# Scan of a chunked delta rule: float16 splits of state, values and updates made in halves of two heads

## The chip, the cores and the metric

The kernel runs on one core of a Trainium2 chip. The metric is the device time of one execution in microseconds (us), the median of several runs. The engines are called PE (TensorE matmul), PEld (TensorE weight load), DVE (VectorE), ACT (ScalarE), POOL (GpSimd) and SP (SyncE, here the queue that issues most transfers).

## The reference

One inference layer over 128 context tokens and 2048 latent tokens, model width 1024. Each token is normalised, modulated and projected; three branches of width 512 mix the tokens, are gated, projected and merged. The change is in branch A, a bidirectional gated delta rule with 4 heads of 128 x 128 state:

```python
def step(s, inp):
    u0_, w_, qk_, qg_, kd_, gl_ = inp
    u = u0_ - jnp.einsum('bhck,bhkv->bhcv', w_, s)
    o = jnp.einsum('bhck,bhkv->bhcv', qg_, s) + jnp.einsum('bhij,bhjv->bhiv', qk_, u)
    s = gl_[..., None, None] * s + jnp.einsum('bhck,bhcv->bhkv', kd_, u)
    return s, o
...
o_f, s_f = gated_delta_chunked(q, k, v, g[:, :, 0], beta[:, :, 0], s0_f)
o_b, s_b = gated_delta_chunked(rev(q), rev(k), rev(v), rev(g[:, :, 1]), rev(beta[:, :, 1]), s0_b)
```

`u0_` and `w_` come from a triangular solve within a chunk.

## The kernel before, in words

Every product is made in float16 pairs: an operand is written as a high part (`hi`, its cast) and a low part (`lo`, the remainder), and `mm3` (through `mm`, line 161, the line of nearly all TensorE rows) adds hi x hi, hi x lo and lo x hi. `split` (lines 900 to 902) makes such a pair from a float32 tile of 128 x 512, which holds four heads of 128 columns: ScalarE casts all of it (line 901), then VectorE makes the remainder of all of it (line 902).

`scan` runs 34 steps: 17 chunks of 128 tokens forward (`d` = 0), then 17 backward (`d` = 1), the context's chunk first in each. A step is a chain through four engines:

- `kT_` (tile `sk`) times the state pair `S16` goes to a PSUM bank; VectorE subtracts it from the values `v_` (tile `sv`), one head at a time (line 973); `split` gives `v16`.
- `v16` times `R`, the chunk's inverse, goes to a bank; VectorE multiplies by beta (line 995); `split` gives `u`.
- `kn16` times `u` goes to a bank; VectorE adds it to the decayed state `S`, one head at a time (line 1012); `split` gives the next `S16`.

In the profile the tiles carry names without digits: `v`, `u`, `S`, `kn` and `sk`. Beside the chain, `level` makes `R` for later chunks, `attend` the outputs `o`, and `finish` normalises them. In the first direction no split of S follows the last chunk; in all there are 34 splits of v, 34 of u and 32 of S.

The scan is a generator. `Pace` (lines 306 to 335) advances it while the weight products of the other branches and of the merge are written out, so that those cover the chain. The order in the program is then changed once more: the kernel is built under a scheduler that works out by its own timing which instruction each engine takes next (`schedule_with_timeline_sim=True`). On the chip each engine runs its list in that order and waits at its head.

Two other users of ScalarE's queue matter. `converting` loads a weight block (tile `wst`) and squares it (line 209) for its scale, then casts it (line 218, `whi` or `bhi`); VectorE makes the remainder (line 219). `branch_block` casts another branch's rows (line 1334, tile `big`), which arrive by transfer too.

Of the kernel before, what the change touches and what calls it, by code (L numbers as in the profile page):

```python
# [11 lines left out]
F16 = mybir.dt.float16  # L12
I32 = mybir.dt.int32
BF16 = mybir.dt.bfloat16
AF = mybir.ActivationFunctionType
ALU = mybir.AluOpType
# [4 lines left out]
P = 128  # L21
# [6 lines left out]
H = 4  # L28
WB = 512
# [8 lines left out]
FS = 4096.0  # L38
# [73 lines left out]
def hybrid_flow_kernel(ctx: ExitStack, tc: tile.TileContext, x_prompt, x_sample, state_delta, c, c_ctx, ln_g, w_ada,  # L112
# [3 lines left out]
    V, A, G, PE, SY = nc.vector, nc.scalar, nc.gpsimd, nc.tensor, nc.sync  # L116
    uid, rot = [0], [0]

    def nm(s):
        uid[0] += 1  # L120
        return f"{s}_{uid[0]}"

    def pool(stack, name, bufs, **kw):
        return stack.enter_context(tc.tile_pool(name=name, bufs=bufs, **kw))

    def sb(pl, shape, tag, dt=F32, bufs=None):
        kw = {} if bufs is None else {"bufs": bufs}
        return pl.tile(list(shape), dt, tag=tag, name=nm(tag), **kw)
# [11 lines left out]
    def bank(pl, shape, tag="b"):  # L140
        if pl is ps_d:
            rot[0] += 1
            pl = ps_d[rot[0] % 3]
        return pl.tile(list(shape), F32, tag=tag, name=nm(tag))
# [18 lines left out]
    def mm3(out, l, r):  # L163

        mm(out, l[0], r[0], True, False)
        mm(out, l[0], r[1], False, False)
        mm(out, l[1], r[0], False, True)
# [224 lines left out]
    for blk in range(8):  # L392
# [3 lines left out]
        ps = bank(ps_d, [2, 256])  # L396
# [41 lines left out]
    for ti, (t0, tn) in enumerate(TBS):  # L438
# [13 lines left out]
        for k in range(KT):  # L452
            ps = bank(ps_d, [P, tn])
            for j in range(nt):
                PE.transpose(ps[:, j * P:(j + 1) * P], xt[:, j, k * P:(k + 1) * P], ident)
            t = sb(p0p, [P, tn], "xm", bufs=3)
# [3 lines left out]
        for g in range(4):  # L460
            ps = bank(ps_d if tn == P and g % 2 else ps_mm, [P, tn])
# [12 lines left out]
    def h3(ap):  # L474
        return ap.rearrange("p (h x) -> p h x", h=H)
# [5 lines left out]
    beta, eg, egl, ed, neg = [sb(dp, dsh, n_) for n_ in ("beta", "eg", "egl", "ed", "neg")]  # L481
# [5 lines left out]
    dq = pool(dl, "dqa", 1, side="right")  # L487
# [118 lines left out]
    for ct in range(12):  # L606
        w = getw(1, 2 if ct < 6 else min(4, 15 - ct))
        for half in range(1):
# [4 lines left out]
            for t0, tn in TBS:  # L613
                flip[0] ^= 1
                ps = bank(ps_d if flip[0] else ps_mm, [P, tn])
                gemm_T(ps, w, 0, xh[:, :, t0:t0 + tn], xl[:, :, t0:t0 + tn])
                o = t0 + 1 if t0 < NS else t0 + 3
# [31 lines left out]
    hs = lambda h: slice(h * P, (h + 1) * P)  # L649
# [4 lines left out]
    def bc(col, n):  # L654
        return col.rearrange("p (h o) -> p h o", o=1).to_broadcast([P, H, n])
# [241 lines left out]

    pair = lambda t_, h: (t_[:, 0, hs(h)], t_[:, 1, hs(h)])

    def split(t_, src, scale=1.0):  # L900
        A.activation(t_[:, 0, :], src, AF.Copy, scale=scale)
        V.scalar_tensor_tensor(t_[:, 1, :], src, scale, t_[:, 0, :], ALU.mult, ALU.subtract)

    def attend(d, t, S, u, qk_, qT_):
        o = sb(dq, [P, WB], "o")
        if S is not None:
            ps = bank(ps_out, [P, WB])
            for h in range(H):
                mm3(ps[:, hs(h)], pair(qT_, h), pair(S, h))
            for h in range(H):  # L910
                A.activation(o[:, hs(h)], ps[:, hs(h)], AF.Copy, scale=eg[:, d, t, h:h + 1])
        yield 1
        ps = bank(ps_out, [P, WB])
        for h in range(H):
            mm3(ps[:, hs(h)], pair(qk_, h), pair(u, h))
        if S is not None:
            for h in range(H):
                V.scalar_tensor_tensor(o[:, hs(h)], ps[:, hs(h)], rq[:, t, h:h + 1], o[:, hs(h)], ALU.mult, ALU.add)
        else:
            V.tensor_tensor(h3(o), h3(ps), bc(rq[:, t, :], P), ALU.mult)  # L920
        yield 1
        if d == 0:
            SY.dma_start(ofD[t], o)
        else:
            yield from finish(t, o)

    def scan():
        order = [(d, s_, t) for d in range(2) for s_, t in enumerate([16] + (list(range(16)) if d == 0 else list(range(15, -1, -1))))]

        def step_loads(i):  # L930

            if i == len(order):
                return None
            d, s_, t = order[i]
            kT_ = None
            if s_:
                kT_ = sb(dq, [P, 2, WB], "sk", F16)
                SY.dma_start(kT_, kTD[t])
            kn_ = sb(dq, [P, WB], "skn")
            SY.dma_start(kn_, kvD[t][:, 0, :])  # L940
            v_ = sb(dq, [P, WB], "sv")
            SY.dma_start(v_, kvD[t][:, 1, :])
            return kT_, kn_, v_

        loaded = step_loads(0)
        lev = level(0, 16)
        R = next(lev)
        for _ in range(14):
            yield 1
        for i in range(3):  # L950
            next(lev)
            if i == 1:
                nlev = level(*order[1][::2])
                R2 = next(nlev)
            for _ in range(3):
                yield 1
        att = iter(())
        for i_, (d, s_, t) in enumerate(order):
            if s_ == 0:
                S = S16 = None  # L960
                S0 = sb(dq, [P, WB], "S")
                SY.dma_start(h3(S0), state_delta[0, 0, d].rearrange("h k v -> k h v"))
            kT_, kn_, v_ = loaded
            G.tensor_tensor(h3(kn_), h3(kn_), bc(ed[:, d, t, :], P), ALU.mult)
            kn16 = sb(dq, [P, 2, WB], "kn16", F16)
            A.copy(kn16[:, 0, :], kn_)
            G.tensor_tensor(kn16[:, 1, :], kn_, kn16[:, 0, :], ALU.subtract)
            if S is not None:
                ps = bank(ps_chain, [P, WB])
                for h in range(H):  # L970
                    mm3(ps[:, hs(h)], pair(kT_, h), pair(S16, h))
                for h in range(H):
                    V.scalar_tensor_tensor(v_[:, hs(h)], ps[:, hs(h)], neg[:, d, t, h:h + 1], v_[:, hs(h)], ALU.mult, ALU.add)  # L973
            v16 = sb(dq, [P, 2, WB], "v16", F16)
            split(v16, v_)
            next(lev, None)
            yield 1
            next(att, None)
            yield 1
            next(nlev, None)  # L980
            yield 1
            next(lev, None)
            yield 1
            next(att, None)
            yield 1
            qk_ = sb(dq, [P, 2, WB], "sqk", F16)
            qT_ = None
            if S is not None:
                qT_ = sb(dq, [P, 2, WB], "sq_", F16)
                SY.dma_start(qT_, qTD[t])  # L990
            SY.dma_start(qk_, qkD[d][t])
            ps = bank(ps_chain, [P, WB])
            for h in range(H):
                mm3(ps[:, hs(h)], [R[:, h, l].rearrange("p b c -> p (b c)") for l in range(2)], pair(v16, h))
            V.tensor_tensor(h3(v_), h3(ps), bc(beta[:, d, t, :], P), ALU.mult)
            u = sb(dq, [P, 2, WB], "u", F16)
            split(u, v_)
            yield 1
            next(nlev, None)
            yield 1  # L1000
            next(att, None)
            yield 1
            last = s_ == 16
            S2 = S216 = None
            if not last:
                ps = bank(ps_chain, [P, WB])
                for h in range(H):
                    mm3(ps[:, hs(h)], pair(kn16, h), pair(u, h))
                if S is not None:
                    S2 = S  # L1010
                    for h in range(H):
                        V.scalar_tensor_tensor(S2[:, hs(h)], S[:, hs(h)], egl[:, d, t, h:h + 1], ps[:, hs(h)], ALU.mult, ALU.add)
                else:
                    st = sb(dq, [P, WB], "of")
                    A.activation(st, ps, AF.Copy, scale=bnds[:, 3:4])
                    SY.dma_start(new_state[0, 0, d].rearrange("h k v -> k h v"), h3(st))
                    S2 = S0
                    V.tensor_scalar(S2, S2, us, FS, ALU.mult, ALU.mult)
                S216 = sb(dq, [P, 2, WB], "S16", F16, bufs=2)
                split(S216, S2, 1.0 / FS)  # L1020
            yield 1
            next(nlev, None)
            lev, nlev = nlev, level(*order[i_ + 2][::2]) if i_ < 32 else iter(())
            loaded = step_loads(i_ + 1)
            R3 = next(nlev, None)
            yield 1
            yield 1
            for _ in att:
                pass
            yield 1  # L1030
            att = attend(d, t, S16, u, qk_, qT_)
            S, S16, R, R2 = S2, S216, R2, R3
        for _ in att:
            yield 1
# [111 lines left out]
    ps = bank(ps_x, [P, 4, P])  # L1146
# [21 lines left out]
    for t in range(NCH):  # L1168
        ps = bank(ps_mm, [P, 4, P])
# [30 lines left out]
    for g in range(4):  # L1200
# [5 lines left out]
        for ti, (t0, tn) in enumerate(TBS):  # L1206
            st = vrow[:, t0:t0 + tn]
            ps = bank(ps_mm, [P, tn])
# [17 lines left out]
    for g in range(4):  # L1226
        xw, zw = getw(2, 2)
        for gh in range(1):
# [18 lines left out]
            for q in range(0, NCH, 4):  # L1247
                qn = min(4, NCH - q)
                ps = bank(ps_mm, [P, qn, P])
                for i in range(qn):  # L1250
                    t = q + i
# [42 lines left out]
            for q4 in range(5):  # L1294
# [8 lines left out]
                if q4 == 2:  # L1303
                    ps = bank(ps_x, [P, P])
# [180 lines left out]
    for i_, t in enumerate(order):  # L1485
# [11 lines left out]
        for i, (c0, c1) in enumerate([(0, 512), (512, 896), (896, D)] if end else [(0, 512), (512, D)]):  # L1497
            cs = slice(c0, c1)
            ps = bank(ps_mm, [P, c1 - c0])
# [53 lines left out]
```

## Time and profile before

| | |
|---|---|
| median of 3 runs | 2205.27 us (2204.06 to 2205.95) |
| profiled execution | 2200.86 us, span 2199.1 us |
| mean granted TensorE clock | 0.994 |
| PE busy | 2135.7 us, 97% |
| DVE, ACT, POOL busy | 59%, 46%, 32% |
| the scan | about 900 to 1720 us |

A row of a group gives line, engine, operation, tiles out<-in, shapes and count, then busy time, mean ns of one, and the idle time of the engine just before with what ended it. A row of a timeline gives the start in us, the duration in us, engine, line, operation, tiles, shapes and count, and in brackets the idle time before it. Matmuls overlap, so the distance between starts, not the duration, is what one costs.

### The profile page before, as it was taken

How to read it: one execution, taken by the hardware profiler on the slowest of the kernel's cores; microseconds unless marked ns; L12 is line 12 of the kernel's file. 1: busy time of each engine (PE TensorE's matmuls, PEld its weight loads, DVE VectorE, ACT ScalarE, POOL GpSimd, SP SyncE). 2: the span in 40 equal slices, each digit the busy share in tenths (PEclk: the TensorE clock that was granted, in tenths of full speed). 3: DMA queues.
4: the chain of work that ended last, by engine and by line, in shares of the span. 5: the costliest groups of instructions: out<-in, count | busy, mean ns of one | idle time of the engine just before them, and what ended most of it. 6: DMA issues, size and time to landing. Idle time of an engine off the chain costs nothing.

```text
span 2199.1 us, 41985 instructions
## 1 busy us (share of the span) xinstructions
PE 2135.7 (97%) x15990; PEld 1232.4 (56%) x15990; DVE 1299.4 (59%) x3085; ACT 1006.6 (46%) x2325; POOL 713.9 (32%) x861
## 2 busy tenths in 40 slices
PE   7999999999899999999899999999999999999998
PEld 3564444455455588878555556555655444444444
DVE  5736755479879696455665555756574544233454
ACT  3545644455555563344644445655653422222332
POOL 1421433223334322432321223355443222122553
PEclk8999999999999999999999999999999999999999
DMA  8434733176777754433755556756664544333542
GB/s 281 145 94 162 253 111 110 60 214 212 243 224 233 209 161 115 118 122 115 220 175 164 163 160 189 240 183 209 213 203 147 172 125 128 119 101 118 174 151 105
DMA packets 304275, 365.04 MB, mean 166 GB/s; under 512 B 39393, under 2 KB 215754, under 8 KB 302026
## 3 DMA queue, kind: packets, MB, share of 16 engines
q1 hardware_dynamic: 251690, 267.38, 39.8%
q0 software_dynamic: 12688, 51.27, 6.5%
q10 hardware_dynamic: 39696, 43.72, 6.0%
q8 instruction: 125, 2.05, 0.4%
q14 instruction: 76, 0.62, 0.1%
HBM read 234.67 MB, written 127.62 MB: 165 GB/s over the span
## 4 chain that ended last, share of the span: by engine, by line
PE 48%; DMA 7%; DVE 4%; ACT 4%; issue 2%; POOL 1%; ACTq 1%; SPq 0%; POOLq 0%; DVEq 0%
PE b L161 47%; DMA wst<-in_w_branch_dram 1%; DMA st<-br 1%; DMA wst<-in_w_in_dram 1%; ACTq L672 1%; POOL st L1133 1%; DMA br<-o 1%; DMA skn<-kv 0%; DMA ei<-XB 0%; DVE sv L973 0%; DVE wlo L219 0%; ACT big L1334 0%; DMA mrow<-mrg 0%; ACT nd L739 0%; DMA XB<-nd 0%
## 5 line engine op out<-in xcount | busy, mean ns | idle before, releaser
L161 PE MATMUL b<-xh,whi 128*128 128x512 f16 (+1 forms) x1920 | 649.5, 347 | 4.7 <-DVE sg L1123 3.0
L161 PE MATMUL b<-xl,whi 128*128 128x512 f16 (+1 forms) x1920 | 650.0, 347 | 0.0
L161 PE MATMUL b<-xh,wlo 128*128 128x512 f16 (+1 forms) x1920 | 649.2, 347 | 0.2 <-DVE wlo L219 0.2
L161 PEld LDWEIGHTS <-whi 128*128 128x128 f16 x3904 | 355.9, 98 | 330.3 <-issue 8.7
L161 PEld LDWEIGHTS <-wlo 128*128 128x128 f16 x1952 | 190.8, 98 | 178.6 <-issue 0.7
L161 PE MATMUL b<-big,bhi 128*128 128x512 f16 (+1 forms) x960 | 250.8, 348 | 1.0 <-DVE big L1335 1.0
L1374 POOL TENSOR_TENSOR mrow<-mrow,sg 128x512 f32<-128x512 f32 (+1 forms) x80 | 94.4, 1181 | 291.8 <-DVE sg L1373 162.4
L161 PE MATMUL b<-big,blo 128*128 128x512 f16 (+1 forms) x480 | 163.4, 348 | 0.0
L1364 ACT ACTIVATE sg<-b,winv 128x512 f32<-128x512 f32 (+1 forms) x120 | 74.2, 618 | 154.7 <-PE b L161 154.2
L161 PEld LDWEIGHTS <-xh 128*128 128x128 f16 x1496 | 118.3, 98 | 30.7 <-issue 2.5
L628 POOL TENSOR_TENSOR cy<-cy,raw 128x545 f32<-128x545 f32 (+1 forms) x48 | 74.3, 1575 | 184.4 <-ACT raw L627 184.4
L161 PEld LDWEIGHTS <-bhi 128*128 128x128 f16 x960 | 87.1, 98 | 75.6 <-issue 0.2
L175 DVE CAST wscb<-wss 128x1 bf16<-128x1 f32 x93 | 14.3, 154 | 192.8 <-ACT wlo L209 88.2
L1373 DVE SCALAR_TENSOR_TENSOR sg<-b,binv,sg 128x512 f32<-128x512 f32 (+1 forms) x80 | 53.4, 668 | 105.6 <-PE b L161 91.1
L858 POOL COPY T<-ES 32x256 f16<-32x256 f16 x68 | 29.1, 427 | 211.9 <-DMA ES<-ei 186.2
L161 PE MATMUL b<-whi,xh 128*128 128x128 f16 x544 | 94.5, 221 | 0.8 <-DVE sg L1123 0.8
L161 PE MATMUL b<-whi,xl 128*128 128x128 f16 x544 | 94.5, 221 | 0.0
L161 PE MATMUL b<-wlo,xh 128*128 128x128 f16 x544 | 94.5, 221 | 0.0
L161 PE MATMUL b<-wohi,mh 128*128 128x512 f16 (+2 forms) x248 | 91.9, 372 | 2.0 <-ACT mh L1441 2.0
L209 ACT ACTIVATE wlo<-wst 128x1024 f16<-128x1024 f32 x52 | 54.9, 1056 | 81.7 <-DMA wst<-in_w_in_dram 68.5
L161 PE MATMUL b<-wohi,ml 128*128 128x512 f16 (+2 forms) x248 | 91.7, 372 | 0.3 <-DVE mscb L175 0.3
L161 PE MATMUL b<-wolo,mh 128*128 128x512 f16 (+2 forms) x248 | 91.9, 372 | 0.0
(455 smaller groups left out, 4302.7 us busy)
## 6 DMA issues: line engine op xcount, KB each, us to landing
wst<-in_w_in_dram SPq DMA_DIRECT2D x60, 512.0 KB, 5.5
qkv<-cy POOLq DMA_DIRECT2D x12, 1089.0 KB, 5.2
st<-br SPq DMA_DIRECT2D x48, 256.0 KB, 5.5
mrow<-mrg SPq DMA_DIRECT2D x18, 512.0 KB, 3.7
mrow<-mrg SPq DMA_DIRECT2D x16, 576.0 KB, 4.3
mrg<-mrow POOLq DMA_DIRECT2D x16, 576.0 KB, 3.5
dc<-dec SPq DMA_DIRECT2D x17, 512.0 KB, 6.1
kq<-qkv SPq DMA_DIRECT2D x34, 256.0 KB, 5.2
```

The source lines that it names most:

```text
L161: PE.matmul(out, l, r, start=start, stop=stop)
L175: V.tensor_copy(sb16, ss)
L209: A.activation(w.lo, st, AF.Square, accum_out=ss)
L628: G.tensor_tensor(y[:, c0:c1], y[:, c0:c1], raw[:, 1 + c0:1 + c1], ALU.mult)
L672: A.dma_start(dst, src)
L858: G.tensor_copy(T16[rows(a0, b), :, :, b], ES[0:32, :, 2 * a0 + b, :, wT])
L1133: G.tensor_tensor(o, sg, src, ALU.mult)
L1364: A.activation(sg, ps, AF.Sigmoid, scale=gw.inv)
L1373: V.scalar_tensor_tensor(sg, ps, binv[:, 1:2], sg, ALU.mult, ALU.mult)
L1374: G.tensor_tensor(mr, mr, sg, ALU.add)
```

## The change

`split` takes a function `make` that makes the source of one head. It calls it for the heads in turn and, after each second head, casts the two finished heads (256 columns); after the four heads it makes the remainder in two halves. The callers hand over their VectorE work as that function: `less` for the values, `weighed` for the updates (their product with beta is now made for two heads at a time), `decayed` for the state. So each 512-wide cast and remainder becomes two of 256, and the product with beta becomes two. `v16` and `u` are allocated as before, ahead of the split.

```diff
-    def split(t_, src, scale=1.0):
-        A.activation(t_[:, 0, :], src, AF.Copy, scale=scale)
-        V.scalar_tensor_tensor(t_[:, 1, :], src, scale, t_[:, 0, :], ALU.mult, ALU.subtract)
+    def split(t_, src, make, scale=1.0):
+
+        for h in range(H):
+            make(h)
+            if h % 2:
+                c = slice((h - 1) * P, (h + 1) * P)
+                A.activation(t_[:, 0, c], src[:, c], AF.Copy, scale=scale)
+        for c in (slice(0, 2 * P), slice(2 * P, 4 * P)):
+            V.scalar_tensor_tensor(t_[:, 1, c], src[:, c], scale, t_[:, 0, c], ALU.mult, ALU.subtract)
...
-                for h in range(H):
+            v16 = sb(dq, [P, 2, WB], "v16", F16)
+
+            def less(h):
+                if S is not None:
                     V.scalar_tensor_tensor(v_[:, hs(h)], ps[:, hs(h)], neg[:, d, t, h:h + 1], v_[:, hs(h)], ALU.mult, ALU.add)
-            v16 = sb(dq, [P, 2, WB], "v16", F16)
-            split(v16, v_)
+
+            split(v16, v_, less)
...
-            V.tensor_tensor(h3(v_), h3(ps), bc(beta[:, d, t, :], P), ALU.mult)
             u = sb(dq, [P, 2, WB], "u", F16)
-            split(u, v_)
+
+            def weighed(h):
+                if h % 2 == 0:
+                    c = slice(h * P, (h + 2) * P)
+                    V.tensor_tensor(v_[:, c].rearrange("p (h x) -> p h x", h=2), ps[:, c].rearrange("p (h x) -> p h x", h=2),
+                                    beta[:, d, t, h:h + 2].rearrange("p (h o) -> p h o", o=1).to_broadcast([P, 2, P]), ALU.mult)
+
+            split(u, v_, weighed)
...
-                    for h in range(H):
-                        V.scalar_tensor_tensor(S2[:, hs(h)], S[:, hs(h)], egl[:, d, t, h:h + 1], ps[:, hs(h)], ALU.mult, ALU.add)
...
-                split(S216, S2, 1.0 / FS)
+
+                def decayed(h):
+                    if S is not None:
+                        V.scalar_tensor_tensor(S2[:, hs(h)], S[:, hs(h)], egl[:, d, t, h:h + 1], ps[:, hs(h)], ALU.mult, ALU.add)
+
+                split(S216, S2, decayed, 1.0 / FS)
```

The scheduler places the instructions of all engines anew from here on. On VectorE, in the same step of the first direction, what makes `u` and what stands around it reads before:

```order
L918 SCALAR_TENSOR_TENSOR o_15096<-b_15168,rq_1398,o_15096 128x128 x4
L995 TENSOR_TENSOR sv_15003<-b_15199,beta_1393 128x512
L874 SCALAR_TENSOR_TENSOR T_1316_10168<-b_15222,T_1316_10168 32x4x32
L902 SCALAR_TENSOR_TENSOR u_15213<-sv_15003,u_15213 128x512
L874 SCALAR_TENSOR_TENSOR R_1315_10166<-b_15222,R_1315_10166 32x4x32 x2
L1370 SCALAR_TENSOR_TENSOR mrow_15037<-b_15266,binv_14752,sg_15264 128x512
L1012 SCALAR_TENSOR_TENSOR S_10714<-S_10714,egl_1395,b_15244 128x128 x4
L902 SCALAR_TENSOR_TENSOR S_1878_15261<-S_10714,S_1878_15261 128x512
```

and now:

```order
L924 SCALAR_TENSOR_TENSOR o_15189<-b_15261,rq_1398,o_15189 128x128 x4
L1009 TENSOR_TENSOR sv_15094<-b_15292,beta_1393 128x256 x2
L908 SCALAR_TENSOR_TENSOR u_15305<-sv_15094,u_15305 128x256 x2
L874 SCALAR_TENSOR_TENSOR T_1316_10168<-b_15318,T_1316_10168 32x4x32
L874 SCALAR_TENSOR_TENSOR R_1315_10166<-b_15318,R_1315_10166 32x4x32 x2
L1036 SCALAR_TENSOR_TENSOR S_10714<-S_10714,egl_1395,b_15340 128x128 x4
L908 SCALAR_TENSOR_TENSOR S_1878_15353<-S_10714,S_1878_15353 128x256
L1388 SCALAR_TENSOR_TENSOR mrow_15128<-b_15364,binv_14836,sg_15362 128x512
L908 SCALAR_TENSOR_TENSOR S_1878_15353<-S_10714,S_1878_15353 128x256
```

The halves of `u` follow one another and have moved ahead of the work on `T`; the row `mrow`, an evacuation of the merge, has moved from ahead of the state's update to between the halves of its remainder. Lines of the changed kernel are higher: 902 is 908, 901 is 906, 995 is 1009, 1012 is 1036, 1370 is 1388.

## The prediction

> **What bounds the kernel now.** I read the page first, then the busy time by stretch.
>
> ```profile
> span 2199.1 us, 41985 instructions
> PE 2135.7 (97%) x15990; PEld 1232.4 (56%) x15990; DVE 1299.4 (59%) x3085; ACT 1006.6 (46%) x2325; POOL 713.9 (32%) x861
> 900.00:1720.00 820.00, 799.96 (x7558) 508.87 (x7557) 474.53 (x1244) 408.72 (x1045) 293.24 (x398) 1.00 0.57 178
> 1060.00:1070.00 10.00, 7.16 (x80) 5.32 (x79) 6.43 (x21) 6.85 (x18) 2.60 (x4) 0.83 0.72 215
> 1400.00:1410.00 10.00, 7.29 (x55) 4.31 (x53) 7.73 (x15) 8.65 (x22) 5.88 (x9) 0.83 0.72 238
> ```
>
> The three last rows give a stretch, then busy time of PE, PEld, DVE, ACT and POOL, then granted clock. TensorE sets the time: 2135.7 of 2199.1 us, and the change leaves its products alone. The scan lies in 900 to 1720 us, where TensorE is idle for 820.0 - 800.0 = 20 us; VectorE and ScalarE are about half busy there. Only that idle time, and what it does to the clock, can move. Twice the clock fell: 0.83 over 10 us is half speed for 3.4 us, a loss of 1.7 us each. The waits of that stretch (total, times, longest):
>
> ```profile
> PE b L161 <- ACT S L901: 4.7, 3, 2.4
> PE b L161 <- DVE Q L889: 3.6, 2, 2.6
> PE b L161 <- DVE S L902: 2.5, 4, 1.1
> PE b L161 <- DVE u L902: 2.1, 2, 1.4
> PE b L161 <- ACT u L901: 2.0, 3, 1.4
> PE b L161 <- ACT v L901: 1.1, 1, 1.1
> PE b L161 <- DVE v L902: 0.8, 2, 0.5
> ```
>
> Lines 901 and 902 are the two halves of `split`. They cost 13.2 us in 15 waits: S 7.2 in 7, u 4.1 in 5, v 1.9 in 3. There are 100 splits (32, 34, 34), so 85 cost nothing. An undisturbed step shows why (start, duration, engine, line, operation; in brackets the idle time before it):
>
> ```profile
> 1248.78 0.22 PE L161 MATMUL b<-v,R 128*128 128x128 f16 x1
> 1249.04 0.69 DVE L995 TENSOR_TENSOR sv<-b,beta 128x512 f32<-128x512 f32 x1 [0.78 <-PE b L161]
> 1249.98 0.63 ACT L901 ACTIVATE u<-sv 128x512 f16<-128x512 f32 x1
> 1250.64 0.69 DVE L902 SCALAR_TENSOR_TENSOR u<-sv,u 128x512 f16<-128x512 f32 x1 [0.37 <-ACT u L901]
> 1254.45 0.22 PE L161 MATMUL b<-u,kn 128*128 128x128 f16 x1
> 1255.16 0.78 PE L161 MATMUL b<-u,kn 128*128 128x128 f16 x11
> 1255.97 1.12 DVE L1012 SCALAR_TENSOR_TENSOR S<-S,egl,b 128x128 f32<-128x128 f32 x4 [3.71 <-PE b L161]
> 1257.13 0.63 ACT L901 ACTIVATE S<-S 128x512 f16<-128x512 f32 x1 [0.41 <-DVE S L1012]
> 1257.79 0.79 DVE L902 SCALAR_TENSOR_TENSOR S<-S,S 128x512 f16<-128x512 f32 x1
> 1259.60 0.22 PE L161 MATMUL b<-S,sk 128*128 128x128 f16 x1
> ```
>
> u is whole at 1251.33, and TensorE comes to it at 1254.45: 3.1 us of cover, made of weight products. S is whole at 1258.58, wanted at 1259.60: 1.0 us of cover. A wait arises where a queue is blocked. The longest:
>
> ```profile
> 1114.71 0.63 ACT L209 ACTIVATE blo<-wst 128x512 f16<-128x512 f32 x1 [6.12 <-DMA wst<-in_w_branch_dram]
> 1115.34 0.60 ACT L966 CAST kn<-skn 128x512 f16<-128x512 f32 x1
> 1116.42 0.61 ACT L901 ACTIVATE S<-S 128x512 f16<-128x512 f32 x1
> 1117.09 0.22 PE L161 MATMUL b<-S,sk 128*128 128x128 f16 x1 [2.35 <-ACT S L901]
> 1445.27 1.06 ACT L209 ACTIVATE wlo<-wst 128x1024 f16<-128x1024 f32 x1 [3.40 <-DMA wst<-in_w_in_dram]
> 1446.32 0.61 ACT L901 ACTIVATE u<-sv 128x512 f16<-128x512 f32 x1
> ```
>
> ScalarE stands 6.12 us before a weight's square (line 209) for that weight's transfer, and the cast of S is queued behind it; at 1445 us the cast of u. So it is less a slow split than one queued behind a late transfer.
>
> **The change part by part.** *Durations.* No row shows a half split. The nearest rows:
>
> ```profile
> L901 ACT ACTIVATE u<-sv 128x512 f16<-128x512 f32 x34 | 21.2, 624 | 29.7 <-DVE sv L995 28.5 <-PE b L161 1.1
> L1282 ACT COPY us<-b 128x256 f32<-128x256 f32 x9 | 3.3, 370 | 8.0 <-PE b L161 8.0
> L1334 ACT ACTIVATE big<-st,bsc 128x128 f16<-128x128 f32 x8 | 3.2, 403 | 4.2 <-DMA st<-br 4.1
> L874 DVE SCALAR_TENSOR_TENSOR R<-b,R 64x256 f16<-64x256 f32 x34 | 14.1, 416 | 12.0 <-ACT R L873 11.5
> L382 DVE SCALAR_TENSOR_TENSOR sg<-wst,scT,sg 128x256 f32<-128x256 f32 x20 | 8.7, 478 | 1.9 <-DMA wst<-in_w_ada_dram 1.9
> L1286 DVE TENSOR_TENSOR yT<-b,us 128x256 f32<-128x256 f32 x7 | 4.2, 602 | 5.9 <-ACT us L1282 5.9
> ```
>
> A half cast is 0.37 to 0.40 us, I take 0.37, the row of its width; a half remainder 0.42 to 0.48, I take 0.43, near the row that also writes float16. The half product with beta lies between 0.42 (the narrowest vector row of that width) and 0.60; I take 0.45, since the 0.60 row writes transposed. Added: ScalarE 100 x (0.74 - 0.62) = 12 us of 820, VectorE 100 x (0.86 - 0.69) + 34 x (0.90 - 0.69) = 24 us, from 475 to 499 of 820. Other work hides this: both stay at 61% or less. Without that cover each wait would bear some 0.2 us, 15 x 0.2 = 3 us; I cost it at nothing.
>
> [...]
>
> *Earlier halves.* From cast start to whole split is now 0.63 + 0.69 = 1.32 us. After, the first pair of heads is whole after 0.37 + 0.43 = 0.80, and its six products cover most of the second pair. So where the cast is late, TensorE starts up to 0.5 us sooner; where the update is late, also by the overlap with the last two updates. Waits shorter than that give only their own length. I take 0.35 us for each of 15: -5.2 us, bounds 0 and -7.5. The other 85 splits gain nothing.
>
> *Where the products stand.* The scheduler places the products anew. TensorE's row at the step quoted above, before:
>
> ```order
> L161 LDWEIGHTS bhi_14691
> L161 MATMUL b_15266<-big_12763,bhi_14691 128x512
> L161 LDWEIGHTS kn_1860_15052
> L161 MATMUL b_15244<-u_15213,kn_1860_15052 128x128
> L161 LDWEIGHTS blo_14692
> L161 MATMUL b_15266<-big_12763,blo_14692 128x512
> ```
>
> and of the changed kernel at the same step:
>
> ```order
> L161 LDWEIGHTS wlo_14348
> L161 MATMUL b_15281<-xh_93,wlo_14348 128x512
> L161 LDWEIGHTS kn_1860_15143
> L161 MATMUL b_15340<-u_15305,kn_1860_15143 128x128
> L161 LDWEIGHTS bhi_14775
> L161 MATMUL b_15364<-big_12803,bhi_14775 128x512
> ```
>
> The first product of u has moved ahead of the branch products of this tile block: 25 full-width products stood between the last product of v and it, now 18. Over all steps the mean falls from 22.8 to 17.6 for u and from 14.9 to 14.4 for S, and rises from 21.9 to 26.8 for v. One takes 0.215 us:
>
> ```profile
> 1252.94 0.38 PE L161 MATMUL b<-xl,whi 128*128 128x512 f16 x1
> 1253.16 0.38 PE L161 MATMUL b<-xh,wlo 128*128 128x512 f16 x1
> 1253.37 0.59 PE L161 MATMUL b<-big,bhi 128*128 128x512 f16 x2
> ```
>
> So u loses 5.2 x 0.215 = 1.1 us of cover: +5.6 us if its five waits all lengthen (none if the new places are free of blocks, the bounds). S loses 0.1 us: 7 x 0.1 = +0.7. v gains 1.05 us of cover, which ends its waits: -1.9. Sum +4.4 us: the split's gain is largely handed back.
>
> *Where ScalarE's conversions stand.* Its order at the 2.35 us wait, before:
>
> ```order
> L218 ACTIVATE bhi_13423<-wst_13112,wsc_13495 128x512
> L209 ACTIVATE blo_14037,wss_14038<-wst_13776 128x512
> L966 CAST kn_1677_13558<-skn_13524 128x512
> L1364 ACTIVATE sg_13596<-b_13509,winv_13123 128x512
> L901 ACTIVATE S_1664_13479<-S_10714 128x512
> L888 ACTIVATE Q_10176<-b_13581 64x256
> ```
>
> and after, at the same step of the scan:
>
> ```order
> L218 ACTIVATE bhi_13477<-wst_13159,wsc_13551 128x512
> L972 CAST kn_1677_13614<-skn_13580 128x512
> L906 ACTIVATE S_1664_13529<-S_10714 128x256 x2
> L209 ACTIVATE blo_14105,wss_14106<-wst_13839 128x512
> L1382 ACTIVATE sg_13654<-b_13565,winv_13170 128x512
> L888 ACTIVATE Q_10176<-b_13639 64x256
> ```
>
> The waiting square now stands behind the casts of S, so this wait goes (-2.35) and the square blocks v instead, which has most cover. In the second direction the reverse happens: there the squares stood ahead of u, and in four steps they now stand ahead of S. A wait for S averages 7.2 / 7 = 1.0 us, one for u 4.1 / 5 = 0.8: four steps at 0.2 to 2.35 us each, and I take 0.25, the difference of the means: +1.0. Sum -1.4.
>
> *The queues.* SP's weight and scan loads change places with each other; no load is added. POOL's work is the same.
>
> **Sum.** -5.2 + 4.4 - 1.4 = -2.2 us against a profiled execution of 2200.86 us (span 2199.1). The median, 2205.27, lies 4.4 above that execution; I set the difference against the median: 2203.1 us. About 0.2%, or 4.4 us, is what a measurement of this kernel can tell from no change.
>
> **The rivals.**
> - *The waits go for good.* If the new places carry no block, the 15 waits shrink to a third (-8.8). For it: one long wait loses its cause, and v's have cover. Against: u's cover fell by 1.1 us in every step. Time 2196.5. A fallen clock that stays up would add 1.7: 2194.8.
> - *A square ahead of S holds TensorE (slower).* Four steps of the second direction at the 2.35 us of the row above, instead of 1.0: +9.4, less the -5.2 of the halves, plus one more stretch at half clock, 1.7: +5.9, 2211.2 us. It decides from the point where a weight lands over 1.0 us (S's cover) later than the scheduler's place for it. For it: ScalarE waited 3.40 and 6.12 us for such transfers. Against: many squares stand ahead of v now.
> - *The halves start nothing sooner.* If the first product of u or S in effect waits for both halves, the -5.2 goes and +3.0 is left: 2208.3 us. For it: some first halves have other casts between them and the second. Against: today TensorE already waits apart for line 901 and line 902.
>
> The clock's fall is judged by the trace: at 1060 to 1070 us the longest wait was 2.6 us, and the clock was halved. [...]
>
> **How the numbers follow.** The forecast, within 4.4 us of the median, 0.37; halves that start nothing sooner 0.10; waits gone 0.30; a square ahead of S 0.23. The first two are within 0.2%: 0.47. The range leaves out a tenth at each end: down to 2195.5, near the first rival with the clock kept, up to 2212.0, just past the second.
>
> **What would show it.** In the profile after: TensorE busy near 2135.7, its idle time in the scan near 18 us; half casts near 0.37 us; no wait for v; waits for S or u still behind line 209 in ScalarE's queue, at other steps. It is wrong if TensorE's idle time in the scan falls under 15 us or passes 25, if a wait by a transfer shows on TensorE itself, or if the difference lies outside the scan.

## The result, and the profile after

| | before | after |
|---|---|---|
| median (lowest to highest), same chip, 19 runs each | 2204.78 us (2200.78 to 2207.82) | 2209.02 us (2203.88 to 2215.05) |
| ratio, 95% interval | | 1.0021 (1.0013 to 1.0030) |
| profiled execution; its span | 2200.86; 2199.1 us | 2213.02; 2211.2 us |

The change costs 0.21%, about 4.6 us. The forecast was 2203.1 us, no measurable change. The two profiled executions lie on opposite sides of their medians, 4 us below and 4 us above, so the traces differ by 12 us and not by 4.6: only what lies in the scan, and what the experiments bear out, is read as the change's.

The page of the changed kernel: the span, and busy time of each engine.

```profile
span 2211.2 us, 42288 instructions
PE 2144.6 (97%) x15990; PEld 1236.1 (56%) x15990; DVE 1325.5 (60%) x3219; ACT 1021.5 (46%) x2425; POOL 718.1 (32%) x861
```

TensorE's products are the same 15990. Its idle time over the whole span is 66.6 us (2211.2 - 2144.6) where it was 63.4. The other 8.9 us (2144.6 - 2135.7) are products that took longer; by the mean granted clocks of the two profiled executions, 0.991 and 0.994, an estimated 7 us of them are the lower clock. The changed kernel by stretch (stretch, length, busy time of PE, PEld, DVE, ACT, POOL, then the granted clock):

```profile
900.00:1720.00 820.00, 793.40 (x7484) 503.62 (x7483) 497.11 (x1356) 419.17 (x1139) 292.52 (x395) 0.99 0.58 176
1060.00:1070.00 10.00, 7.08 (x89) 5.63 (x87) 4.87 (x15) 5.85 (x19) 4.61 (x6) 0.86 0.61 179
1430.00:1450.00 20.00, 16.87 (x122) 9.68 (x121) 10.32 (x29) 10.16 (x29) 7.47 (x11) 0.83 0.63 172
```

In the scan TensorE is idle 820 - 793.4 = 26.6 us, 20.0 before: the 6.6 us are lost there. VectorE's 497.1 and ScalarE's 419.2 us are close to what the prediction added up to (499, and 408.7 + 12 = 421). At two places the clock is halved again, for 2.8 us of the first window (0.86 over 10) and 6.8 us of the second (0.83 over 20). TensorE's waits for the splits and for R from 900 to 1740 us (total, times, longest):

```profile
PE b L161 <- DVE S L908: 5.1, 8, 1.0
PE b L161 <- DVE S L1036: 3.7, 2, 2.5
PE b L161 <- ACT u L906: 3.2, 3, 1.4
PE b L161 <- ACT R L873: 3.1, 5, 1.0
PE b L161 <- ACT S L906: 3.0, 2, 2.5
PE b L161 <- DVE u L908: 0.9, 3, 0.5
PE b L161 <- DVE v L908: 0.6, 1, 0.6
```

u costs 4.1 us as before, v 0.6 instead of 1.9, and S 11.8 us in 12 waits instead of 7.2 in 7. The largest group has doubled: eight waits for the remainder of S (line 908), which cost 2.5 us in 4 before. Not all of the rise is new idle time: 2.5 us of it stand at 1066 us behind a weight's square, at the step at which the kernel before had its 2.6 us for the tile `Q` of `level` (line 889), and the waits for that tile fell from 3.6 to 0.3 us. The groups of line 908, of the casts and of the product with beta, in the scan (engine, operation, tiles and shape, count; busy time, mean ns of one; idle time before them), first the state's remainder of the kernel before and then those of the changed kernel:

```profile
L902 DVE SCALAR_TENSOR_TENSOR S<-S,S 128x512 f16<-128x512 f32 x32 | 27.8, 869 | 10.6 <-ACT S L901 10.3
```

```profile
L908 DVE SCALAR_TENSOR_TENSOR S<-S,S 128x256 f16<-128x256 f32 x64 | 40.5, 656 | 3.2 <-ACT S L906 2.4
L908 DVE SCALAR_TENSOR_TENSOR u<-sv,u 128x256 f16<-128x256 f32 x68 | 31.3, 488 | 10.1 <-ACT u L906 9.6
L906 ACT ACTIVATE u<-sv 128x256 f16<-128x256 f32 x68 | 25.2, 408 | 44.9 <-DVE sv L1009 41.2 <-PE b L161 3.6
L1009 DVE TENSOR_TENSOR sv<-b,beta 128x256 f32<-128x256 f32 x68 | 25.6, 416 | 12.9 <-PE b L161 12.8
```

A half remainder of u takes 0.49 us, one of S 0.66: the same operation, the same width, the same operands' kinds. So it is not the width that costs. What it is, a step of the second direction shows in the timeline of the changed kernel (start, duration, engine, line, operation; in brackets the idle time before it):

```profile
1482.29 0.62 ACT L972 CAST kn<-skn 128x512 f16<-128x512 f32 x1
1482.81 0.72 ACT L906 ACTIVATE S<-S 128x256 f16<-128x256 f32 x2
1483.05 1.15 POOL L973 TENSOR_TENSOR kn<-skn,kn 128x512 f16<-128x512 f32 x1 [0.75 <-ACT kn L972]
1483.25 1.56 DVE L908 SCALAR_TENSOR_TENSOR S<-S,S 128x256 f16<-128x256 f32 x2 [0.21 <-ACT S L906]
1483.27 0.22 PE L161 MATMUL b<-S,sk 128*128 128x128 f16 x1
1484.53 0.77 PE L161 MATMUL b<-S,sk 128*128 128x128 f16 x11 [1.02 <-DVE S L908]
```

The two halves take 1.56 us. TensorE has issued one product of the first head's high part and then stands 1.02 us for its remainder. Beside that remainder POOL makes another one, that of the scan's keys `kn` (line 973), which begins 0.2 us earlier. Before, in the same order on ScalarE (cast of `kn`, then cast of S), here in the first direction:

```profile
1191.18 0.62 ACT L966 CAST kn<-skn 128x512 f16<-128x512 f32 x1 [2.72 <-PE b L161]
1191.95 1.16 POOL L967 TENSOR_TENSOR kn<-skn,kn 128x512 f16<-128x512 f32 x1 [0.50 <-ACT kn L966]
1192.49 0.62 ACT L901 ACTIVATE S<-S 128x512 f16<-128x512 f32 x1
```

There the remainder of S could not begin before 1193.11, when the cast of all four heads ended, and POOL's operation ended at that very time. Casting two heads at a time brings the first remainder forward, into POOL's operation.

Counted piece by piece in the changed kernel's trace: 26 of the 64 halves of S's remainder take over 1.2 times the shortest one's 0.41 us, 15.4 us in excess of it, and 15 of the 26 begin inside POOL's remainder of `kn`. Before, 9 of 32 take over 1.2 times the shortest whole one's 0.68 us (excess 5.3 us), 4 of them begun inside that of `kn`. And of TensorE's waits for S, six (3.6 us) fall on a stretched piece that is still running, one (1.1 us) before.

### The profile page after: what moved, and what is told of

The parts are those of the page before. It is cut to its first block, busy times and chain, and to the rows that moved or that the text cites. A ratio compares the mean times of both kernels' runs of the same rounds, so it can differ in the third digit from the quotient of the medians.

```text
span 2211.2 us, 42288 instructions
## 1 busy us (share of the span) xinstructions
PE 2144.6 (97%) x15990; PEld 1236.1 (56%) x15990; DVE 1325.5 (60%) x3219; ACT 1021.5 (46%) x2425; POOL 718.1 (32%) x861
## 4 chain that ended last, share of the span: by engine, by line
PE 49%; DMA 6%; DVE 4%; ACT 3%; issue 2%; POOL 1%; ACTq 1%; SPq 1%; POOLq 0%; DVEq 0%
PE b L161 48%; DMA st<-br 1%; DMA wst<-in_w_branch_dram 1%; ACTq L672 1%; DMA wst<-in_w_in_dram 1%; DMA mrow<-mrg 0%; DVE S L908 0%; ACT big L1352 0%; DMA mrg<-mrow 0%; DVE big L1353 0%; DVE S L1036 0%; ACT o L917 0%; DMA XB<-nd 0%; DMA sv<-kv 0%; DMA br<-o 0%
## 5 line engine op out<-in xcount | busy, mean ns | idle before, releaser
L219 DVE SCALAR_TENSOR_TENSOR wlo<-wst,wsc,whi 128x1024 f16<-128x1024 f32 x52 | 73.1, 1408 | 31.3 <-ACT whi L218 31.0
```

The costliest lines, as they stand in the source:

```text
L219: V.scalar_tensor_tensor(w.lo, st, s, w.hi, ALU.mult, ALU.subtract)
```

## Experiments

The expectations speak of three theories. **P**: the halves of S's remainder, earlier than the whole one was, meet POOL's remainder of `kn` and stretch. **Q**: weights' squares now stand ahead of the casts of S and hold TensorE (the prediction's slow rival). **L**: the scheduler's new placement alone, a lottery in which the halves have no part. All ratios are to the kernel before on the same chip, with their 95% intervals.

**S whole, v and u in halves.** `whole` is the old split with the source made first.

```diff
+    def whole(t_, src, make, scale=1.0):
+        for h in range(H):
+            make(h)
+        A.activation(t_[:, 0, :], src, AF.Copy, scale=scale)
+        V.scalar_tensor_tensor(t_[:, 1, :], src, scale, t_[:, 0, :], ALU.mult, ALU.subtract)
...
-                split(S216, S2, decayed, 1.0 / FS)
+                whole(S216, S2, decayed, 1.0 / FS)
```

> The changed kernel with the state split whole again (v and u stay in halves). Theory P (the earlier halves of the state's remainder run into POOL's remainder of kn and stretch): the remainder of S falls back from 40.5 us of VectorE time in the scan to about 28, waits for S from 11.8 to about 7 us, the time to 2203 to 2206. Theory Q (weight squares stand ahead of the cast of S by the scheduler's new order): time follows where squares stand in the new order, 2204 to 2211, and the waits for S that stay begin behind line 209. Theory L (any re-placement scatters the time): anywhere from 2200 to 2212, without a link to the remainder of S.

**S in halves, v and u whole.**

```diff
-            split(v16, v_, less)
+            whole(v16, v_, less)
...
-            split(u, v_, weighed)
+            V.tensor_tensor(h3(v_), h3(ps), bc(beta[:, d, t, :], P), ALU.mult)
+            whole(u, v_, lambda h: None)
```

> The kernel before with the state split alone in halves (v and u whole). P: the cost comes with S, so waits for S of 10 us or more and 2207 to 2211. Q: as e1, by the squares ahead of S. L: 2200 to 2212 with no link.

Measured: 1.0013 (1.0002 to 1.0024) with S whole, 1.0039 (1.0025 to 1.0052) with only S in halves. S in halves alone is the slowest of the three, and with S whole 0.13% of loss is left: S's part carries most of it, but the parts do not add up (0.13 and 0.39 against 0.21%). The groups of the first kernel, the waits of TensorE in the last column:

```profile
L914 DVE SCALAR_TENSOR_TENSOR S<-S,S 128x512 f16<-128x512 f32 x32 | 28.2, 881 | 10.4 <-ACT S L913 9.9
L161 PE MATMUL b<-S,sk 128*128 128x128 f16 x384 | 32.5, 221 | 2.1 <-DVE S L914 1.7 <-ACT S L913 0.3
L161 PE MATMUL b<-u,kn 128*128 128x128 f16 x384 | 32.0, 219 | 8.6 <-ACT u L906 5.0 <-DVE u L908 3.5
```

and the second's:

```profile
L908 DVE SCALAR_TENSOR_TENSOR S<-S,S 128x256 f16<-128x256 f32 x64 | 36.9, 605 | 4.5 <-ACT S L906 4.1
```

With S whole its waits fall to 2.0 us and its remainder is back at 0.88 us, but the waits for u rise from 4.1 to 8.5: halves of u do not protect u once its products move. With S alone in halves the remainder is stretched as P says, yet only 1.3 of the 9.3 us of waits for S fall on a stretched piece, and 6.0 are three waits behind weights' squares. P alone does not make this kernel the slower of the two; Q has its share.

**`kn` prepared later.** The four lines that prepare `kn` (POOL's product, its remainder, the cast) stand behind the split of v in the code, in the changed kernel and in the one before.

```diff
-            G.tensor_tensor(h3(kn_), h3(kn_), bc(ed[:, d, t, :], P), ALU.mult)
-            kn16 = sb(dq, [P, 2, WB], "kn16", F16)
-            A.copy(kn16[:, 0, :], kn_)
-            G.tensor_tensor(kn16[:, 1, :], kn_, kn16[:, 0, :], ALU.subtract)
...
             split(v16, v_, less)
...
+            G.tensor_tensor(h3(kn_), h3(kn_), bc(ed[:, d, t, :], P), ALU.mult)
+            kn16 = sb(dq, [P, 2, WB], "kn16", F16)
+            A.copy(kn16[:, 0, :], kn_)
+            G.tensor_tensor(kn16[:, 1, :], kn_, kn16[:, 0, :], ALU.subtract)
```

> The changed kernel with the preparation of kn (ScalarE cast, POOL remainder) written one stage later, behind the split of v, so POOL's remainder of kn no longer stands beside the state's split. P: halves of S near 0.42 us each instead of 0.66, 27 to 31 us of VectorE time, and 2201 to 2206. Q: the squares stay ahead of S, 2207 to 2211. L: 2200 to 2212.

> The kernel before with the same later preparation of kn. P: the remainder of S falls from 27.8 to about 23 us, the time by 0 to 3 us, less than in e3. Q: about the same as before. L: 2200 to 2212.

Measured: 1.0027 (1.0018 to 1.0037) and 1.0007 (0.9994 to 1.0019). The edit missed its aim: the scheduler put the work on `kn` back ahead, and S's remainder stayed stretched:

```profile
L908 DVE SCALAR_TENSOR_TENSOR S<-S,S 128x256 f16<-128x256 f32 x64 | 40.0, 646 | 3.3 <-ACT S L906 2.6
```

It says nothing for or against P; as a rewriting of the same program that moves either kernel by under 0.1% it is one sample of L.

**No remainder of `kn`.**

```diff
-            kn16 = sb(dq, [P, 2, WB], "kn16", F16)
-            A.copy(kn16[:, 0, :], kn_)
-            G.tensor_tensor(kn16[:, 1, :], kn_, kn16[:, 0, :], ALU.subtract)
+            kn16 = sb(dq, [P, WB], "kn16", F16)
+            A.copy(kn16, kn_)
...
-                    mm3(ps[:, hs(h)], pair(kn16, h), pair(u, h))
+                    mm3(ps[:, hs(h)], (kn16[:, hs(h)], kzero[:, hs(h)]), pair(u, h))
```

> The changed kernel without POOL's remainder of kn (left out: the low part of kn is a fixed tile of zeros; TensorE's products stay as many). P: with nothing of kn on POOL the halves of S's remainder take 0.42 to 0.5 us each, 27 to 32 us in all instead of 42, waits for S fall from 11.8 to 4 to 8 us, time 2200 to 2205, and the gap to e6 is -2 to +2 us. Q and L: the halves get faster too, but the gap to e6 stays near +4 us.

> The kernel before without POOL's remainder of kn (left out in the same way). P: S's remainder falls from 28 to about 24 us, time 2200 to 2204. Q and L: 2199 to 2205.

Measured: 0.9989 (0.9977 to 1.0000) in the changed kernel, 0.9988 (0.9978 to 0.9998) in the kernel before: the difference between the two is gone. S's half remainder falls from 656 to 519 ns:

```profile
L908 DVE SCALAR_TENSOR_TENSOR S<-S,S 128x256 f16<-128x256 f32 x64 | 32.0, 519 | 2.8 <-ACT S L906 1.9
```

The times are as P has them. The waits for S in the profiled run, 9.1 us, are not what P expected; 2.9 of them still fall on a piece stretched by other POOL work.

**`kn`'s remainder on VectorE.** One line, in both kernels: the operation stays, POOL is out of it.

```diff
-            G.tensor_tensor(kn16[:, 1, :], kn_, kn16[:, 0, :], ALU.subtract)
+            V.tensor_tensor(kn16[:, 1, :], kn_, kn16[:, 0, :], ALU.subtract)
```

> The changed kernel with the remainder of kn on VectorE instead of POOL; nothing is left out. P: S's halves no longer share their time with POOL's work on kn, 0.42 to 0.55 us each, but kn's remainder (some 0.7 us) stands in VectorE's own queue; time 2201 to 2207 and the gap to e10 -2 to +2 us. Q and L: the gap stays near +4, or anything from -6 to +8.

> The kernel before with the remainder of kn on VectorE. P: within 3 us of before, since before only 4 of 32 remainders of S met kn's. Q: the same.

Measured: 0.9989 (0.9980 to 0.9997) in the changed kernel, 1.0031 (1.0018 to 1.0045) in the kernel before. In the changed kernel:

```profile
900.00:1720.00 820.00, 801.22 (x7551) 507.94 (x7550) 509.48 (x1408) 419.67 (x1142) 258.35 (x364) 0.99 0.58 177
L908 DVE SCALAR_TENSOR_TENSOR S<-S,S 128x256 f16<-128x256 f32 x64 | 31.5, 521 | 0.8 <-ACT S L906 0.4
L973 DVE TENSOR_TENSOR kn<-skn,kn 128x512 f16<-128x512 f32 x34 | 24.9, 731 | 8.3 <-ACT kn L972 4.3 <-PE b L161 2.0 <-issue 1.9
```

VectorE is given 25 us more, and gets back 9 of them in S's remainder; TensorE's idle time falls from 26.6 to 18.8 us. With `kn` on VectorE the halves are 0.42% faster than the whole split. But the kernel before became slower by the same edit, although its own remainder of S shortened too (869 to 792 ns), so part of that 0.42% is placement. For the kernel before P had expected a time within 3 us; it is 7 us longer.

**S's cast in halves, its remainder in one piece.** `split` is given the pieces of the remainder.

```diff
-    def split(t_, src, make, scale=1.0):
+    def split(t_, src, make, scale=1.0, parts=(slice(0, 2 * P), slice(2 * P, 4 * P))):
...
-        for c in (slice(0, 2 * P), slice(2 * P, 4 * P)):
+        for c in parts:
...
-                split(S216, S2, decayed, 1.0 / FS)
+                split(S216, S2, decayed, 1.0 / FS, (slice(0, 4 * P),))
```

> The changed kernel, S cast in halves but its remainder made in one piece, which can begin only behind the second cast. P: it starts some 0.4 us later than the first half did and meets kn's remainder once, not twice: S's remainder 28 to 34 us, time 2203 to 2207. Q: as after, 2207 to 2211, if the squares keep their places. L: 2200 to 2212.

Measured: 2200.25 us, 0.9985 (0.9975 to 0.9995), faster than both kernels, and than the 2203 us at least that P had for it:

```profile
900.00:1720.00 820.00, 802.79 (x7584) 509.91 (x7585) 491.89 (x1352) 422.58 (x1147) 293.05 (x398) 1.00 0.59 178
L908 DVE SCALAR_TENSOR_TENSOR S<-S,S 128x512 f16<-128x512 f32 x32 | 27.5, 859 | 8.2 <-ACT S L906 7.9
L161 PE MATMUL b<-S,sk 128*128 128x128 f16 x384 | 32.0, 219 | 6.7 <-DVE S L908 3.4 <-ACT S L906 2.8 <-DVE S L1036 0.6
```

TensorE's idle time is 17.2 us. The waits for S are 6.7 us instead of 11.8, and those on a stretched piece 0.3 us instead of 3.6. The remainder is still held now and then: 13 of 32 are stretched, 10 of them over `kn`, but by 5.5 us in all instead of 15.4. By place the squares stand ahead of S as in the changed kernel, at the same three steps. Yet the one that ScalarE came to at 1436.9 us there, after 3.35 us for its transfer, is not late here (0.02 us), and the waits for S behind squares are 2.9 us instead of 6.2. So this kernel by itself does not separate P from Q.

The same with `kn`'s remainder on VectorE:

```diff
-            G.tensor_tensor(kn16[:, 1, :], kn_, kn16[:, 0, :], ALU.subtract)
+            V.tensor_tensor(kn16[:, 1, :], kn_, kn16[:, 0, :], ALU.subtract)
...
-                split(S216, S2, decayed, 1.0 / FS)
+                split(S216, S2, decayed, 1.0 / FS, (slice(0, 4 * P),))
```

> The changed kernel with kn's remainder on VectorE and S's remainder in one piece. P: with nothing of kn on POOL one piece or two is the same, so within 2.5 us of the two pieces (ratio to before 0.998 to 1.000), where on POOL one piece gained some 8 us. L: any distance from -8 to +8 us.

and with all three remainders in one piece, `kn` on POOL:

```diff
-        for c in (slice(0, 2 * P), slice(2 * P, 4 * P)):
+        for c in (slice(0, 4 * P),):
```

> The changed kernel with all three remainders in one piece behind halved casts. P: most of the gain is S's, so within 3 us of the kernel with S's remainder alone in one piece, ratio to before 0.997 to 1.000. L: 0.997 to 1.004.

Measured: 0.9984 (0.9973 to 0.9994) and 0.9992 (0.9981 to 1.0002). Four kernels now form a square, with v and u in halves and all S casts in halves:

| ratio to before | S's remainder in two pieces | in one piece |
|---|---|---|
| `kn`'s remainder on POOL | 1.0021 (the change) | 0.9985 |
| `kn`'s remainder on VectorE | 0.9989 | 0.9984 |

Two pieces cost 0.36% where POOL works on `kn`, and 0.05%, within the intervals, where it doesn't. The cut by itself does not give this pattern; P does. Against Q speaks the kernel with both edits: TensorE waits for S behind the same three squares for 6.1 us, as in the changed kernel, and it is as fast as any. L is not excluded, since each of the four kernels is a placement of its own.

**Squares later.** A `yield` ahead of each weight's square of the later weights, in both kernels, was to let other work pass the square.

```diff
+        if wnext[0] > 24:
+            yield
```

> The changed kernel with each later weight's square written one stage later, so that its transfer has some 3 to 5 us more. Q: ScalarE's idle time ahead of line 209 falls from some 70 to under 35 us in the scan, waits for S fall from 11.8 to 4 to 7 us and the gap to e8 closes to -2 to +2 us. P: waits for S stay at 8 to 12 us, the gap at +3 to +6. L: any gap from -6 to +8.

> The kernel before with the same later squares. Q: its 13 us of waits for splits fall to 4 to 8, time 2198 to 2203. P: the same, since the one long wait for S begins behind a square. L: 2199 to 2210.

Measured: 1.0087 (1.0073 to 1.0100) and 1.0037 (1.0024 to 1.0050). A failed experiment: ScalarE's idle time ahead of line 209 did not fall (74.8 us in the scan, 73.6 in the changed kernel without the `yield`), the waits for S stayed at 11.3 us, and TensorE's idle time in the scan rose to 32.9 and 28.5 us. It does not test Q.

**Another pace.** The constant that sets how much filling work the planner lays beside each step of the scan is raised by 1.5%, which places all products anew. Three kernels: before, the change, and the change with S's remainder in one piece.

```diff
-SCAN = 1.3
+SCAN = 1.32
```

> The kernel before with its pace of the scan at 1.32 instead of 1.30 us a stage: no instruction is added, removed or resized, all of the scan is placed anew. L: the time moves by 3 us or more. P and Q: under 2.5 us unless squares or kn happen to meet S.

> The changed kernel at a pace of 1.32 us instead of 1.30: the whole scan placed anew. P: the two pieces meet kn in this placement too: S's remainder 36 us or more, slower than before by 0.1 to 0.5%. L: ratio anywhere from 0.998 to 1.004, unlinked to the remainder.

> The same pace with S's remainder in one piece. P: S's remainder under 30 us, and faster than e14 by 3 to 9 us. L: faster or slower than e14 with equal chance.

Measured: 1.0011 (1.0001 to 1.0020), 1.0038 (1.0026 to 1.0050) and 1.0025 (1.0012 to 1.0037). The change is slower than before here too, by 0.27%. One piece is better than two by only 0.13%, with intervals that overlap, and is here slower than the kernel before. In the profile of the change at this pace S's remainder is stretched as ever,

```profile
L908 DVE SCALAR_TENSOR_TENSOR S<-S,S 128x256 f16<-128x256 f32 x64 | 39.1, 628 | 11.0 <-ACT S L906 10.4
```

yet the waits for S are 4.7 us, fewer than in the kernel before, 1.9 of them on a stretched piece, and the largest wait is another one, for `o`:

```profile
PE b L1067 <- ACT o L1063: 7.2, 5, 3.5
```

So in the five profiles with two pieces of S and `kn` on POOL the halves average 0.60 to 0.66 us; what that costs depends on whether TensorE's products of S are due just then. The gain of the one-piece version, 0.15% at one pace, does not carry over to another, where it is 0.14% slower than the kernel before (1.0025 against 1.0011).

**What is shown and what stays open.** Shown: two pieces of S's remainder are stretched by POOL's work, most of it goes when POOL's remainder of `kn` (a half from 0.656 us to 0.519 and 0.521) or the second piece goes (15.4 us of excess to 5.5), and at this pace the sign of the change goes with it. In the traces the waits on stretched pieces account for 3.6 - 1.1 = 2.5 us of the 6.6 us of added idle time. Open: whether the stretch is what turns the sign, or the new placement that comes with each edit; how much of the rest is stretched VectorE work that delays something else; and how much is squares whose transfers come late. Edits that only place anew moved the time by 0.06 and 0.07% (`kn` prepared later), by 0.11, 0.17 and 0.40% (the pace, in the kernel before, the change and the one-piece version); that is the size of the whole effect.

## Why the prediction was wrong

- **Earlier halves, -5.2 us: the step that failed.** A half remainder was sized 0.43 us, near the row of line 874. That row reads one operand from a PSUM bank (`b`): 9 of its 34 operations began inside a POOL operation, and all 34 took 0.41 to 0.42 us. The remainder of S has both operands in SBUF. Undisturbed it takes 0.41 to 0.43 us too, but it measured 0.656 on average. For S the sum had -2.45 from earlier halves, +0.7 from places and -1.4 from squares, together -3.1 us; its waits rose by 4.6 us, 2.5 of them on stretched pieces. The prediction looked at what runs on ScalarE and VectorE at the new, earlier time, and said of POOL only that its work is the same. The work is, but its neighbour is not.
- **Hidden at nothing.** Right for the totals, which are at 497 and 419 us, VectorE's by luck: S's remainder took 12.7 us more (40.5 - 27.8) where 32 x 0.17 = 5.4 were added, the product with beta 2.3 us more where 7.1 were. Wrong for S, which has 1.0 us of cover and whose remainder took 0.4 us more per split (2 x 0.656 against 0.869).
- **Sizes.** A half cast measured 0.41 us (taken 0.37, from the row of a copy out of PSUM), a half product with beta 0.416 (0.45). Two half casts in a row overlap (0.72 us for two at 1482.81), so ScalarE's total does not show the difference.
- **Where the products stand, +4.4 us.** For u the sum had +5.6 from places and -1.75 from earlier halves; its waits stayed at 4.1 us, so the two cancelled, at sizes that this run does not tell apart. That places can cost u more, the kernel with S whole shows: 8.5 us. For v the direction is right, from 1.9 to 0.6, but the sum took its three waits off twice, as -1.9 here and as 3 x 0.35 among the 15. For S, +0.7 was too little.
- **The long wait behind a square, -1.4 us.** It went, as forecast: the square moved behind the casts. The other half of that step, squares that now stand ahead of S, was given 1.0 us. In the second direction two such waits cost 3.7, besides the one at 1066 us. The timeline of the changed kernel at the longer:

```profile
1436.91 0.63 ACT L209 ACTIVATE blo<-wst 128x512 f16<-128x512 f32 x1 [3.35 <-DMA wst<-in_w_branch_dram]
1437.54 0.60 ACT L972 CAST kn<-skn 128x512 f16<-128x512 f32 x1
1437.66 0.16 DVE L175 CAST wscb<-wss 128x1 bf16<-128x1 f32 x1 [3.79 <-ACT blo L209]
1437.84 1.12 DVE L1036 SCALAR_TENSOR_TENSOR S<-S,egl,b 128x128 f32<-128x128 f32 x4
1438.47 0.93 ACT L906 ACTIVATE S<-S 128x256 f16<-128x256 f32 x2 [0.33 <-DVE S L1036]
1439.10 0.22 PE L161 MATMUL b<-S,sk 128*128 128x128 f16 x1 [2.48 <-DVE S L1036]
1439.54 1.81 DVE L908 SCALAR_TENSOR_TENSOR S<-S,S 128x256 f16<-128x256 f32 x2
1439.70 1.37 POOL L1392 TENSOR_TENSOR mrow<-mrow,sg 128x512 f32<-128x512 f32 x1 [0.26 <-DVE sg L1391]
1441.40 0.69 PE L161 MATMUL b<-S,sk 128*128 128x128 f16 x5 [0.60 <-DVE S L908]
```

- **The slow rival** thus did happen, here and at 1508 us (1.23 us), by way of VectorE's queue as much as ScalarE's: VectorE stood 3.79 us for the square before the small cast of line 175, and the update of S was queued behind that. The stretch with halved clock came with it, around the wait of 2.48 us; it lasts 6.8 us and costs 3.4, where the rival had 1.7. Its mechanism is real; that it does not turn the sign by itself rests on the kernel with both edits, which waits as long behind these squares and is fast. The same rows show the other mechanism: POOL's evacuation of the merge holds the second half, and TensorE waits a second time. The rival's own sum left out the +4.4 and the -2.35 of the forecast: with them it is +7.95 instead of +5.9, 2213.2 us, outside the stated range.
- **What was to prove it wrong**, idle time in the scan past 25 us, did: 26.6.

## What to carry to other kernels

Before an operation is cut so that a part of it starts sooner, look at what every other engine does at that new time, POOL above all: of the 45 half remainders, both operands in SBUF, that began inside an element-wise POOL operation other than line 171's with over 0.2 us of it to go, 41 here took 0.53 to 1.49 us instead of 0.41, and ended 0.27 to 0.28 us after a POOL operation had. Cutting only the operation on the engine that is late (the cast, on ScalarE) and leaving the other whole gained 0.15% at one pace; at the other it did not. In a kernel whose scheduler places everything anew, a difference of 0.2% is read from pairs of kernels under more than one placement, not from one pair.

## What the runs showed of the hardware

A half remainder that takes 0.41 us alone took up to 1.49 us beside POOL. In the scan of the changed kernel 41 halves of S, v and u are stretched; every one of them began after a POOL operation had begun, and ended 0.27 to 0.28 us after a POOL operation's end, whatever its length (0.39 to 2.04 us). Of the 17 halves that began while POOL was free and had a POOL operation begin beside them, none was stretched. The rows at 1439.54 and 1439.70 show both: the first half began 0.16 us ahead of POOL's operation and took 0.41 us, the second met it and took 1.48. A held whole remainder of the kernel before ended 0.54 to 0.55 us after POOL's operation (15 of 100). So of the 0.41 us of a half, and of the 0.69 of a whole one, most comes only after that end, and the profile shows the time in which the piece is held as busy time of VectorE, not as a wait.

POOL's operations took longer too. In the kernel before, its additions of line 1374 take 1.27 us (the median of those that no remainder precedes); the four of 128 x 512 that began inside a whole remainder took 1.57 to 1.71. This one began 0.10 us into it:

```profile
1569.14 0.68 DVE L902 SCALAR_TENSOR_TENSOR v<-sv,v 128x512 f16<-128x512 f32 x1
1569.24 1.71 POOL L1374 TENSOR_TENSOR mrow<-mrow,sg 128x512 f32<-128x512 f32 x1 [1.13 <-DVE wsc L183]
```

Not every overlap holds a piece. Ten halves of the changed kernel that began inside POOL's operation of line 171, on 128 x 4 values, with over 0.2 us of it to go, were not stretched. Nor were three second halves that followed their first directly (at 1370.1, 1596.2 and 1674.3 us), although POOL had begun 0.01 to 0.17 us earlier; there POOL's operation took longer instead, 1.34, 1.71 and 1.56 us, where the medians of their lines are 1.04, 1.27 and 1.27. So which of the two is held is not told by the order of their starts alone. And the updates of S, which read one operand from a PSUM bank, were not held: 47 of the 120 began inside an element-wise POOL operation other than line 171 with over 0.2 us of it to go, and the longest of all 120 takes 0.35 us.

```profile
L1036 DVE SCALAR_TENSOR_TENSOR S<-S,egl,b 128x128 f32<-128x128 f32 x120 | 33.7, 341 | 12.3 <-PE b L161 11.9
```

The clock was halved for 6.8 us (0.83 over 20 us, 0.50 from 1440 to 1446 us) around a wait of 2.48 us. In the kernel before it was halved for 3.4 us (0.83 over 10 us, 0.50 from 1066 to 1068 us) around one of 2.6 us, and stayed whole (1.00 from 1110 to 1130 us) around one of 2.35 us at 1117 us.
